# A hybrid attention layer on one core: the place of every instruction written down instead of found by priority

## The chip, the cores and the metric

The kernel runs on one core of a Trainium2 chip. The metric is the device time of one launch in microseconds (us), the median over several runs. The engines are TensorE (PE, matmuls and transposes; its weight loads are drawn apart as PEld), VectorE (DVE), ScalarE (ACT), GpSimd (POOL) and SyncE (SP), which only issues DMAs. Each engine has an instruction list of its own and takes it strictly in order; semaphores hold an instruction until what it needs is there.

## The reference

One layer on 1024 tokens of 1024 features. Cut to what is computed:

```python
h = rms_norm(x, norm_pre_g)
sb_q, sb_k, sb_v, sb_g, c_q, c_kv, k_rope, mla_g = split(h @ w_in)       # 1024 -> 2976
# group A, 8 heads of 64: stick-breaking attention, blocks of 128 queries, strictly causal
z = q_blk @ k.T * 64 ** -0.5
log_fail = where(past, log_sigmoid(-z), 0)
suffix = cumsum(log_fail, reverse=True) - log_fail
w = where(past, exp(log_sigmoid(z) + suffix), 0);  sb_o = w @ v
# group B, 8 heads: latent attention
q = rms_norm(c_q, q_norm_g) @ w_uq;  kv = rms_norm(c_kv, kv_norm_g) @ w_ukv
z = (q_nope @ k_nope.T + rope(q_rope) @ rope(k_rope).T) * 96 ** -0.5
mla_o = softmax(where(visible, z, -inf)) @ v
y = concat(head_rms_norm(sb_o) * silu(sb_g), head_rms_norm(mla_o) * silu(mla_g)) @ w_out
x = x + rms_norm(y, norm_post_g)
x = x + rms_norm(p @ w_ple, ple_norm_g) * sigmoid(x @ w_ple_gate + b_ple_gate)
```

Everything is float32.

## The kernel before

*Arithmetic and tiles.* A float32 product is made of three matmuls: each operand is split into a high part (a cast to the rounded type fp32r) and a low part (a subtraction), and high x high, high x low and low x high are added in one PSUM bank. So nearly every matrix that PE reads has first been cast (on ACT or DVE) and subtracted (on DVE or POOL). Matmuls are up to 512 columns wide; 128x128 transposes stand between them. q, k, v, the gates and other intermediate results go through DRAM scratch (`q_d`, `k_d`, `v_d`, `qr_d`, `gate_d`, `ple_d`), so a later stage reads by DMA what an earlier one stored.

*Stages.* The head (to about 20 us) loads x and the weights of v. Then come the projections by blocks of 128 tokens or 128 columns, woven with attention from about 65 us on. Attention is worked off in 16 rounds (`SEQ`: a head pair of one of the two groups, for one half), its matmuls woven with the remaining projections. From about 560 us on come the output projection, the second norm, and the last product with `w_ple_gate`, made by seven block products instead of eight; the tail is the last sum, sigmoid, product, addition and store of the output.

*What sets the order.* The kernel isn't written engine by engine. The calls of `block_kernel` go to a `Recorder`, which notes 6621 instructions with their dependences: PE 3905, SP 386 DMAs, the rest on DVE, ACT and POOL. `FLIP` is a list of numbers of such instructions that go to another engine than the text says (`other`): a `tensor_tensor` from DVE to POOL or back, a copy from ACT to DVE or back. `schedule` then plays the program through with estimated durations and gives each instruction a time; `issue` emits them in the order of those times, so that all of them have the same line in the profile (L754 before, L1069 after). The list that results is fixed when the kernel is built. Nothing is decided on the chip.

*Buffers.* Tiles come from pools that rotate: 28 places `u` and 10 places `f` of 4 KB per partition in SBUF, the four `h16`, and in PSUM 3 banks `a` (accumulators) and 5 banks `t` (transposes, scores). In the profile and in the rows below a tile is named by its place: `u_11` is the eleventh of `u`. A tile gets its place in `grant` in the order of the tiles' `turn`; a place is free when the last user of the earlier tile is done, a storing DMA included. So an instruction can wait for its inputs, for the engine that used its output's place before, or for the instructions ahead of it on its own engine.

*The priority before.* Of the instructions that are ready on an engine `schedule` takes the one with the lowest `prio`: its number in the program's text, plus a shift of its chunk (`SHIFT`, one pair of numbers for each piece of the program, the first for instructions and the second for tiles), plus `LOW` for the filling work, plus a bias.

Of the kernel before, what the change touches and what calls it, by code (L numbers as in the profile page):

```python
# [47 lines left out]
def f(ap):  # L48
# [4 lines left out]
LOW = 336  # L53
# [22 lines left out]
SHIFT = {  # L76
# [267 lines left out]
SETS = {AF.Sigmoid: "sig", AF.Exp: "exp", AF.Sin: "sin"}  # L344


class Recorder:
# [3 lines left out]
    def __init__(self, nc):  # L351
# [4 lines left out]
        self.low = False  # L356
        self.front = False
        self.bias = 0
        self.chunk = 0
        self.thread = ""  # L360
        self.threads = [""]

# [7 lines left out]
    def tile(self, pool, shape, dt, tag, slots, name, kind, part=None):  # L370
# [9 lines left out]
        key = t.tensor.name  # L380
# [19 lines left out]
    def turn(self, by=0):  # L400
        return len(self.ins) + SHIFT.get(self.chunk, (0, 0))[by]

# [1444 lines left out]
```

## Time and profile before

| | |
|---|---|
| time, median of 3 runs | 767.02 us (766.11 to 768.51) |
| the profiled execution | 765.48 us |
| its span in the trace | 763.7 us |
| PE busy | 751.0 us, 3905 matmuls and transposes |
| DVE, ACT, POOL busy | 630.6, 399.7, 321.7 us |
| DMA traffic | 148.71 MB, 195 GB/s over the span |
| granted clock of PE, mean | 0.999 |

The profiled execution lies 1.5 us below the median, and 1.8 us of it are outside the span that the trace shows. Busy times are sums of what each engine shows as running; a matmul is drawn from its start to a modelled end, so neighbours overlap and a short hold of PE inside a run doesn't appear as idle time. Idle time of an engine other than PE costs nothing by itself.

### The profile page before, as it was taken

How to read it: one execution, taken by the hardware profiler on the slowest of the kernel's cores; microseconds unless marked ns; L12 is line 12 of the kernel's file. 1: busy time of each engine (PE TensorE's matmuls, PEld its weight loads, DVE VectorE, ACT ScalarE, POOL GpSimd, SP SyncE). 2: the span in 40 equal slices, each digit the busy share in tenths (PEclk: the TensorE clock that was granted, in tenths of full speed). 3: DMA queues.
4: the chain of work that ended last, by engine and by line, in shares of the span. 5: the costliest groups of instructions: out<-in, count | busy, mean ns of one | idle time of the engine just before them, and what ended most of it. 6: DMA issues, size and time to landing. Idle time of an engine off the chain costs nothing.

```text
span 763.7 us, 11831 instructions
## 1 busy us (share of the span) xinstructions
PE 751.0 (98%) x3905; PEld 621.0 (81%) x3905; DVE 630.6 (83%) x1238; ACT 399.7 (52%) x962; POOL 321.7 (42%) x306
## 2 busy tenths in 40 slices
PE   7999999999999999999999999999999999999997
PEld 4888998878888878888887788888888888888876
DVE  6966355599958869888888999989899998789987
ACT  7633133244534785666657767767765541451221
POOL 2141113104411269869888521430363126464642
PEclk9999999999999999999999999999999999999999
DMA  9753103587998643656545884878436367272332
GB/s 324 247 168 129 74 33 120 190 313 279 341 355 272 214 132 137 198 189 209 175 138 162 270 298 145 286 267 286 144 116 212 125 248 244 87 276 83 110 111 83
DMA packets 101982, 148.71 MB, mean 195 GB/s; under 512 B 7448, under 2 KB 55072, under 8 KB 101920
## 3 DMA queue, kind: packets, MB, share of 16 engines
q1 hardware_dynamic: 101920, 147.95, 57.3%
q8 instruction: 31, 0.51, 0.3%
q14 instruction: 31, 0.25, 0.1%
HBM read 101.26 MB, written 46.66 MB: 194 GB/s over the span
## 4 chain that ended last, share of the span: by engine, by line
PE 88%; ACT 5%; DVE 3%; DMA 2%; issue 1%; POOL 0%; SPq 0%; ACTq 0%; DVEq 0%; POOLq 0%
PE a L754 62%; PE t L754 26%; ACT u L754 3%; DVE u L754 1%; DMA u<-k_d 1%; DMA v_d<-f 1%; ACT L754 1%; ACT h L754 1%; ACT f L754 1%; DVE nm L754 1%; DVE f L754 1%; DMA u<-v_d 0%; SPq L754 0%; DVE t L754 0%; DVE nms L754 0%
## 5 line engine op out<-in xcount | busy, mean ns | idle before, releaser
L754 POOL TENSOR_TENSOR u<-u,u 128x512 f32<-128x512 f32 (+14 forms) x134 | 190.5, 1436 | 140.1 <-ACT u L754 74.8
L754 PE MATMUL a<-h,f 128*128 128x512 f32 x864 | 240.7, 404 | 0.0
L754 PEld LDWEIGHTS a<-h,f 128*128 128x128 f32 x864 | 155.2, 189 | 26.4
L754 DVE TENSOR_TENSOR u<-t,u 128x512 fp32r<-128x512 f32 (+4 forms) x284 | 150.6, 555 | 22.2 <-ACT u L754 12.8
L754 PE MATMUL t<-u,u 128*128 128x512 f32 (+4 forms) x580 | 151.0, 367 | 1.0 <-DMA u<-k_d 0.5
L754 PE MATMUL a<-u,u 128*128 128x512 f32 (+2 forms) x522 | 133.4, 370 | 0.1
L754 PE MATMUL t<-ident,u 128*128 128x128 f32 (+1 forms) x793 | 126.4, 273 | 1.4 <-DVE nms L754 0.5
L754 ACT CAST u<-t 128x512 fp32r<-128x512 f32 (+3 forms) x192 | 87.4, 490 | 75.4 <-PE t L754 49.0
L754 PEld LDWEIGHTS t<-u,u 128*128 128x128 f32 x580 | 103.0, 189 | 20.2 <-ACT u L754 3.2
L754 PE MATMUL a<-h,u 128*128 128x512 f32 (+1 forms) x492 | 117.3, 391 | 0.1
L754 ACT ACTIVATE u<-t 128x512 f32<-128x512 f32 (+5 forms) x208 | 92.0, 515 | 47.2 <-PE t L754 38.6
L754 PEld LDWEIGHTS t<-ident,u 128*128 128x128 f32 (+1 forms) x793 | 97.1, 140 | 22.3 <-DVE u L754 2.9
L754 PEld LDWEIGHTS a<-h,u 128*128 128x128 f32 x492 | 89.6, 188 | 20.3 <-DVE u L754 0.5
L754 PEld LDWEIGHTS a<-u,u 128*128 128x128 f32 x522 | 91.7, 188 | 16.9 <-DVE u L754 2.0
L754 DVE TENSOR_TENSOR u<-u,u 128x512 fp32r<-128x512 f32 (+8 forms) x88 | 79.6, 917 | 5.3 <-ACT u L754 3.5
L754 ACT ACTIVATE u<-t,nms 128x384 f32<-128x384 f32 (+5 forms) x96 | 55.2, 581 | 39.7 <-DVE nms L754 39.4
L754 DVE TENSOR_TENSOR_SCAN u<-u 128x320 f32<-128x320 f32 (+4 forms) x64 | 64.6, 1011 | 13.6 <-ACT u L754 12.4
L754 ACT ACTIVATE f<-a 128x512 bf16<-128x512 f32 (+2 forms) x64 | 34.2, 539 | 51.5 <-PE a L754 48.4
L754 POOL MEMSET u<- 128x128 f32 x64 | 13.0, 216 | 102.1 <-PE a L754 56.4
L754 DVE TENSOR_TENSOR u<-a,u 64x512 f32<-64x512 f32 (+4 forms) x75 | 47.8, 647 | 8.2 <-ACT u L754 6.9
L754 DVE TENSOR_REDUCE nm<-t 128x1 f32<-128x384 f32 (+5 forms) x96 | 51.8, 547 | 1.9 <-PE t L754 1.2
L754 PE MATMUL a<-u,h 128*128 128x512 f32 x192 | 47.0, 399 | 1.5 <-ACT h L754 1.4
(111 smaller groups left out, 801.1 us busy)
## 6 DMA issues: line engine op xcount, KB each, us to landing
u<-q_d SPq DMA_DIRECT2D x64, 256.0 KB, 4.4
u<-k_d SPq DMA_DIRECT2D x16, 512.0 KB, 5.1
u<-v_d SPq DMA_DIRECT2D x16, 512.0 KB, 5.4
u<-in_w_ple_gate_dram SPq DMA_DIRECT2D x16, 512.0 KB, 6.7
f<-in_w_in_dram SPq DMA_DIRECT2D x14, 512.0 KB, 5.1
v_d<-u SPq DMA_DIRECT2D x12, 512.0 KB, 3.1
f<-in_x_dram SPq DMA_DIRECT2D x9, 512.0 KB, 4.4
q_d<-u SPq DMA_DIRECT2D x9, 512.0 KB, 4.4
```

The costliest lines, as they stand in the source:

```text
L754: x["fn"](*[place(a) for a in x["args"]], **{k: place(a) for k, a in x["kw"].items()})
```

## The change

`SHIFT` is empty. `FLIP` is a new list. `BASE` holds one number for each of the 6621 instructions, its place, and `TURNS` one for each tile of a rotating pool, its turn; both were found by a search that also played the program with transfers landing late. With `BASE` there, `schedule` no longer picks the lowest ready instruction: each engine's instructions are sorted by `BASE` and taken strictly in that order. No arithmetic, DMA or tile is added or removed.

```diff
-SHIFT = {
-    0: (1204, 1209), 1: (-381, -413), 2: (-586, -394), 3: (-857, -953), 4: (-1159, -1106), 5: (-11, -91),
...
+SHIFT = {}
 FLIP = (
...
+BASE = (
+    3, 5, 8, 4, 2, 6, 10, 7, 17, 18, 19, 21, 22, 24, 26, 28, 29, 33, 36, 38, 14, 15, 23, 57, 13, 16, 44, 87, 56, 60,
...
+TURNS = (
+    2, 18, 16, 17, 16, 81, 159, 162, 141, 189, 273, 274, 275, 161, 192, 182, 393, 378, 372, 142, 145, 71, 80, 80, 71,
...
-            self.tiles[key].update(turn=self.turn(1), turn0=len(self.ins), chunk=self.chunk)
+            self.tagged += 1
+            place = TURNS[self.tagged - 1] if TURNS else len(self.ins)
+            self.tiles[key].update(turn=place + SHIFT.get(self.chunk, (0, 0))[1], turn0=place, chunk=self.chunk)
...
-    def turn(self, by=0):
-        return len(self.ins) + SHIFT.get(self.chunk, (0, 0))[by]
+    def turn(self):
+        i = len(self.ins)
+        return (BASE[i] if BASE else i + (LOW if self.low else 0) + self.bias) + SHIFT.get(self.chunk, (0, 0))[0]
...
-                             chunk=self.chunk, prio=self.turn() + (LOW if self.low else 0) + self.bias, func=SETS.get(func) if op == "activation" else None))
+                             chunk=self.chunk, prio=self.turn(), func=SETS.get(func) if op == "activation" else None))
...
+        line = {e: sorted((i for i in range(n) if ins[i]["eng"] == e), key=lambda i: (-ins[i]["prio"], -i))
+                for e in engines}
         while done < n:
             best = None
             for e in engines:
-                if avail[e]:
+                if BASE:
+                    if not line[e] or need[line[e][-1]]:
+                        continue
+                    s = max(free[e], ready[line[e][-1]])
+                elif avail[e]:
...
-            while pend[e] and pend[e][0][0] <= s:
-                r, i = heapq.heappop(pend[e])
-                heapq.heappush(avail[e], (ins[i]["prio"], i))
-            _, i = heapq.heappop(avail[e])
+            if BASE:
+                i = line[e].pop()
+            else:
+                while pend[e] and pend[e][0][0] <= s:
+                    r, i = heapq.heappop(pend[e])
+                    heapq.heappush(avail[e], (ins[i]["prio"], i))
+                _, i = heapq.heappop(avail[e])
```

Between the two `FLIP` lists 253 instructions change engine: 76 from DVE to ACT, 62 from ACT to DVE, 62 from POOL to DVE, 53 from DVE to POOL. On PE the order moves only locally. Three places are spoken of below. A row gives the line, the operation, its output, its inputs and the output's shape.

*DVE at 65 to 82 us.* Here the weights of `c_load` (two 128-row blocks by 416 columns at a time, 832 columns in a row) are split; `128x832` with two inputs is the subtraction that makes a low part, and `128x4x64` are the casts and subtractions of `v_store`, whose result goes to `v_d`. Before:

```order
L754 SCALAR_TENSOR_TENSOR u_9_782<-u_9_782 128x256
L754 TENSOR_TENSOR u_22_792<-u_22_792 128x192
L754 SCALAR_TENSOR_TENSOR u_22_792<-u_22_792 128x192
L754 CAST f_7_815<-a_1_308 128x4x64
L754 TENSOR_TENSOR u_22_792<-u_22_792 128x382
L754 TENSOR_TENSOR f_7_815<-a_1_308,f_7_815 128x4x64
L754 CAST f_7_815<-a_1_308 128x4x64
L754 TENSOR_TENSOR f_0_826<-f_2_683,f_3_748 128x832
L754 TENSOR_TENSOR f_7_815<-a_1_308,f_7_815 128x4x64
L754 CAST f_8_840<-a_2_235 128x4x64
L754 TENSOR_TENSOR f_8_840<-a_2_235,f_8_840 128x4x64 x2
L754 CAST f_7_872<-f_2_834 128x832
```

The same place after:

```order
L1069 TENSOR_TENSOR f_1_752<-a_2_306,f_1_752 128x4x64 x2
L1069 TENSOR_TENSOR t_1_165<-t_1_165,mask_71 128x128
L1069 TENSOR_TENSOR t_2_173<-t_2_173,mask_71 128x128
L1069 TENSOR_TENSOR t_4_226<-t_4_226,mask_71 128x128
L1069 SCALAR_TENSOR_TENSOR u_14_764<-u_14_764 128x128
L1069 TENSOR_TENSOR f_1_800<-f_2_713,f_6_757 128x832
L1069 SCALAR_TENSOR_TENSOR u_18_783<-u_18_783 128x256
L1069 CAST f_7_813<-a_1_197 128x4x64
```

The subtraction (`f_0_826`, now `f_1_800`) has moved ahead of the scans of 256 and 192 columns (`SCALAR_TENSOR_TENSOR` in these rows) and of the casts of `v_store`, and the cast of the next block, `f_7_872` before, is no longer on DVE. The place `f_1` that it writes was the v tile `f_1_752`, which is being stored to `v_d`.

*PE at 434 to 439 us.* Transposes of softmax rows into `t` banks, and the wide matmuls of weights by values into an `a` bank. Before:

```order
L754 MATMUL t_2_224<-ident_66,u_21_4024 128x128
L754 MATMUL t_2_224<-ident_66,u_24_4101 128x128
L754 MATMUL t_2_224<-ident_66,u_26_4141 128x128
L754 MATMUL t_2_224<-ident_66,u_16_4185 128x128
L754 MATMUL t_1_216<-ident_66,u_24_4101 128x128
L754 MATMUL t_1_216<-ident_66,u_26_4141 128x128
L754 MATMUL t_1_216<-ident_66,u_16_4185 128x128
...
L754 MATMUL a_2_235<-u_27_4316,u_7_3965 128x512 x2
L754 MATMUL a_2_235<-u_20_4307,u_7_3965 128x512 x2
```

After:

```order
L1069 MATMUL a_0_128<-u_27_3815,u_26_4018 128x512
L1069 MATMUL t_2_173<-ident_66,u_4_4033 128x128
L1069 MATMUL t_2_173<-ident_66,u_14_4103 128x128
L1069 MATMUL a_0_128<-u_20_4227,u_26_4018 128x512
L1069 MATMUL t_2_173<-ident_66,u_13_4163 128x128
L1069 MATMUL t_2_173<-ident_66,u_18_4197 128x128
L1069 MATMUL t_0_180<-u_3_4236,u_8_2021 128x256
L1069 MATMUL t_0_180<-u_3_4236,u_20_4227 128x256
L1069 MATMUL t_0_180<-u_7_2023,u_0_4112 128x256
L1069 MATMUL a_0_128<-u_2_2036,u_26_4018 128x512
L1069 MATMUL t_1_165<-ident_66,u_14_4103 128x128
L1069 MATMUL t_1_165<-ident_66,u_13_4163 128x128
```

Value matmuls of the same accumulator, now in bank `a_0` instead of `a_2`, stand between the transposes of `t_2` and `t_1`; before they came after all of them.

*SP at 490 to 495 us.* Loads of a round of latent attention: parts of q (`q_d5`), of v (`v_d1`), of k (`k_d5`), the rotary part of q (`qr_d`), and other work's DMAs. Before:

```order
L754 DMA u_3_3224<-q_d5_91 128x512
L754 DMA u_4_4984<-v_d1_85 128x8x128
L754 DMA u_25_3756<-q_d5_91 128x1x512
L754 DMA u_11_4998<-k_d5_99 128x1024
L754 DMA u_13_4371<-qr_d_102 128x1x512
L754 DMA f_9_5016<-in_w_out_dram 128x2x512
L754 DMA gate_d5_109<-f_7_4538 128x512
```

After:

```order
L1069 DMA u_25_4969<-q_d5_91 128x1x512
L1069 DMA u_18_4976<-q_d5_91 128x512
L1069 DMA u_26_4994<-k_d5_99 128x1024
L1069 DMA u_25_4969<-qr_d_102 128x1x512
L1069 DMA f_9_5006<-in_w_out_dram 128x2x512
L1069 DMA gate_d5_109<-f_0_4658 128x512
L1069 DMA u_0_5036<-v_d1_85 128x8x128
```

The load of v has gone from second place to the last of the seven, and k is third.

More of the change, by code (lines that the diff above doesn't have):

```diff
@@ L74 @@
 AHEAD = 52
-SHIFT = {
[160 rows of a table removed]
-}
-FLIP = (
[11 rows of a table removed]
+SHIFT = {}
+FLIP = (
[13 rows of a table added]
+)
+BASE = (
[341 rows of a table added]
+)
+TURNS = (
[114 rows of a table added]
 )
@@ L359, in __init__ @@
         self.chunk = 0
+        self.tagged = 0
         self.thread = ""
```

636 rows, old and new, of tables (BASE, FLIP, SHIFT, TURNS) are left out of this document.

## The prediction

> **What bounds the kernel now.** I read the head of the page first: the span, the busy engines, the clock and the chain that ended last.
>
> ```profile
> span 763.7 us, 11831 instructions
> PE 751.0 (98%) x3905; PEld 621.0 (81%) x3905; DVE 630.6 (83%) x1238; ACT 399.7 (52%) x962; POOL 321.7 (42%) x306
> PE 88%; ACT 5%; DVE 3%; DMA 2%; issue 1%; POOL 0%; SPq 0%; ACTq 0%; DVEq 0%; POOLq 0%
> ```
>
> TensorE (PE) is busy for 98% of the span and carries 88% of the chain, so a new order can only gain what PE spends standing. How much is that? The windows say where it is plain to see.
>
> ```profile
> 0.00:100.00 100.00, 95.32 (x455) 77.70 (x456) 60.98 (x163) 45.04 (x135) 20.69 (x33) 1.00 0.53 180
> 400.00:500.00 100.00, 97.52 (x544) 80.83 (x543) 93.18 (x220) 70.35 (x181) 44.15 (x41) 1.00 0.71 237
> 700.00:764.00 64.00, 58.54 (x276) 47.73 (x274) 54.48 (x79) 15.15 (x26) 30.72 (x22) 0.98 0.28 100
> ```
>
> After the name and length of a window stand PE, PEld, DVE, ACT and POOL, then the granted clock, 1.00 here. PE idles 763.7 - 751.0 = 12.7 us: 4.7 in the first hundred, 2.5 between 400 and 500, 5.2 in the last window up to the end of the span, and 0.3 in all the rest. That is a lower bound, since a matmul held up for a tenth of a microsecond is still drawn as busy. The upper bound is a count at the unstalled pace, which the chain gives in one long row.
>
> ```profile
> 660.07 23.18 PE a L754 x100
> 683.25 0.55 PE t L754 x5
> ```
>
> The hundred are 512 columns wide: 0.232 us each; a transpose takes 0.11. All forms of matmul, first and last of the 26 rows of that view:
>
> ```profile
> L754 PE MATMUL a<-h,f 128*128 128x512 f32 x864 | 240.7, 404 | 0.0
> ...
> L754 PE MATMUL t<-ident,u 8*128 8x8 f32 x1 | 0.2, 223 | 0.0
> ```
>
> Added up over the 26 rows, 2196 matmuls are 512 wide (509 us), 768 are 256 to 448 wide (123 us in proportion to width), 929 are 128-wide transposes, mask additions and one small one (101 us), and 12 in the head are slow (5.24 us, below): about 738 us, an estimate. The next rows show that the first matmul starts at 2.21 and the last ends at 757.74 + 0.86 = 758.60.
>
> ```profile
> 2.21 5.24 PE a L754 x12
> ```
> ```profile
> 757.74 0.86 PE L754 MATMUL a<-h,u 128*128 128x256 f32 x6
> 758.21 0.93 POOL L754 TENSOR_TENSOR u<-u,u 128x256 f32<-128x256 f32 x1 [0.87 <-ACT u L754]
> 758.64 0.42 DVE L754 TENSOR_TENSOR u<-a,u 128x256 f32<-128x256 f32 x1
> ```
>
> 758.6 - 2.2 - 738 leaves 18 us of standing between first and last matmul, plus 5.1 us of tail. Three or four of the 18 are the head, where weights and x have yet to arrive. So 12 to 14 us is all that any order can take from the middle, most of it in pieces of 0.1 to 0.5 us. Hence I look for the few places with a stall of about one microsecond and ask whether the new order cures them, and what it exposes instead.
>
> **The change, part by part.** Nothing is computed that was not computed before; PE runs the same 3905 matmuls. Every engine executes its list in order, before and after, so what changes is who stands behind whom.
>
> *1. The c_q/c_kv weight at 65 to 82 us (removed: 1.0 us).*
>
> ```profile
> 73.35 1.01 DVE L754 TENSOR_TENSOR f<-f,f 128x832 fp32r<-128x832 f32 x1
> ```
> ```profile
> 74.43 0.38 SPq L754
> ...
> 74.91 6.39 DMA v_d<-f
> ...
> 81.40 0.60 DVE f L754
> ```
> ```profile
> DVE f L754 <- DMA v_d<-f: 5.2, 2, 4.6
> PEld a L754 <- DVE f L754: 1.0, 1, 1.0
> ```
>
> The low part of the first weight block is taken late on DVE (73.35 to 74.36). Only then is its raw buffer free, so the next block's load goes out at 74.43 and the store of v behind it at 74.91. The store lands at 81.30, DVE splits the next block at 81.40, and PE loses 1.0 us. The new order has that subtraction 11 places earlier on DVE, right behind a scan, and gives the next block's cast to ACT. What then holds the subtraction is the landing of an earlier store of v, whose buffer it takes. That store went alone:
>
> ```profile
> GB/s 412 437 409 384 313 209 45 30 0 0 0 0 0 0 0 89 387 447 432 417 134 0 0 0 0 0 0 0 0 0 0 0 0 0 0 0 0 0 0 0
> ```
>
> This is the traffic from 62 to 73 us in 40 slices: the store's packets fill slices 16 to 21, from 66.1 to 67.8. Its four pieces are made later in the new order, by about 1.9 us when I lay the durations of before along the new DVE and ACT rows, so it lands near 69.7. The load then goes out near 71 instead of 74.4 and the second store near 74, which gives 3 us against a stall of 1.0. Between bounds: 0 if the earlier store lands late, -1.0 if not. I take -1.0.
>
> *2. The attention stage at 434 to 438.6 us (removed: 1.4 us).*
>
> ```profile
> 435.47 0.66 PE L754 MATMUL t<-ident,u 128*128 128x128 f32 x4 [0.22 <-DVE u L754]
> 436.67 0.55 PE L754 MATMUL t<-ident,u 128*128 128x128 f32 x3 [0.54 <-DVE nms L754]
> 437.54 0.39 PE L754 MATMUL t<-u,u 128*128 128x256 f32 x1 [0.32 <-ACT u L754]
> ...
> 438.59 2.58 PE L754 MATMUL a<-u,u 128*128 128x512 f32 x10
> ```
> ```profile
> 436.59 0.68 DVE L754 TENSOR_TENSOR f<-a,f 128x512 f32<-128x512 f32 x1
> ...
> 437.85 0.68 DVE L754 TENSOR_TENSOR f<-a,f 128x512 f32<-128x512 f32 x1
> ```
>
> Seven transposes of two softmax rows follow each other at the pace at which DVE and ACT make the rows: 0.22 + 0.54 + 0.32 = 1.08 us idle in the drawing, 1.6 us if the starts are laid against the pace of 0.11 per transpose. Eight wide value matmuls then stand ready but behind, because their accumulator's bank is freed only by the DVE addition at 437.85. In the new order the accumulator has another bank, freed by the addition that was at 436.59, which now stands earlier on DVE, and six of the eight stand between these transposes: 6 x 0.232 = 1.39 us of work over a wait of 1.6. I take -1.4. The other bound is +0.5: if that addition is still late, the first wide matmul waits and with it all transposes behind it.
>
> *3. The load of k at 491 to 499.5 us (removed: 0.8 us).*
>
> ```profile
> 491.11 0.55 SPq L754 DMA_DIRECT2D u<-v_d  x1
> ...
> 492.47 0.53 SPq L754 DMA_DIRECT2D u<-k_d  x1
> ```
> ```profile
> 492.47 6.85 DMA u<-k_d
> ...
> 499.46 1.55 PE t L754 x10
> ```
> ```profile
> PEld t L754 <- issue: 0.8, 1, 0.8
> ```
>
> The load of v (512 KB) stands before k in the queue though v is used well after k. The new order puts v behind k, the rotary queries, a weight of w_out and a gate store. k then goes out near 491.2, 1.3 us earlier, with 512 KB less ahead of it; either alone covers the stall of 0.8. v becomes late instead: issued near 494 and needed after 510, it has 16 us for a transfer that took k 6.85. I take -0.8; bounds 0 and -0.8.
>
> *4. Swaps of engine.* 76 casts go from DVE to ACT and 62 back, 62 products and subtractions from POOL to DVE and 53 back. DVE's count stays nearly the same, but the mix moves with the stage. Prices of the products between 280 and 400 us:
>
> ```profile
> L754 DVE TENSOR_TENSOR u<-t,u 128x512 fp32r<-128x512 f32 x23 | 14.7, 680 | 1.9 <-ACT u L754 1.9
> L754 DVE TENSOR_TENSOR u<-u,u 128x512 fp32r<-128x512 f32 x6 | 8.6, 1429 | 1.3 <-ACT u L754 1.3
> ```
> ```profile
> L754 POOL TENSOR_TENSOR u<-u,u 128x512 f32<-128x512 f32 x10 | 17.8, 1788 | 0.6 <-DMA u<-gate_d 0.5
> ```
>
> With one input in PSUM the operation takes 0.68 us on DVE, with both in SBUF beside a busy POOL 1.43. A product moved from POOL to DVE costs DVE 0.68 to 1.43 us, frees POOL of 1.79 and shortens what DVE runs beside it. Between 280 and 400 this adds about 9 us to DVE by count; DVE has idle time there, and from 560 on, where it is fuller, the swaps take 6 to 7 us off it per hundred. I count the swaps as -1.0 us on the small stalls, between -5 (a third of the 14 us) and +3 (nine products moved to DVE from 685 us on, each late by a third of a microsecond).
>
> The Trainium skill ("SBUF — State Buffer", Who interferes with whom) states that a DVE operation with two SBUF inputs and a GpSimd operation that reads SBUF exclude each other for the whole instruction. The pair 680 and 1429 agrees: 0.75 us is what one such meeting costs here. The rule speaks against the moves to POOL late in the kernel; that case is rival d.
>
> *5. Head and tail (added: 0.5 us).* In the head the casts of the first v weights swap ACT and DVE and x's first block is loaded second rather than fourth. The first weight's low part comes about 1 us later and PE has caught up by 20 us: 0, within 0.6 either way. In the tail the last 256-wide product goes from DVE to POOL. POOL took 0.93 for such a one in the row at 758.21, and DVE 0.42 for an operation as wide at 758.64: +0.5, on the path, since the sum and the store of the output stand behind it.
>
> *Sum.* -1.0 - 1.4 - 0.8 - 1.0 + 0.5 = -3.7 us on a profiled execution of 765.5 us, of which the span is 763.7 and 1.8 lies around it. The median of the runs shown is 767.0, 1.5 us above; I count from the median: 763.3, rounded to 763.
>
> **The rivals.** *a. The stalls move (same).* DVE is the second engine throughout: 93.18 us busy between 400 and 500, with PE behind it all the time. An order fixed in advance may cure three places and open three others of the same size. One I can name: at 688 us.
>
> ```profile
> 687.10 1.21 DVE L754 TENSOR_TENSOR h<-u,h 128x1024 fp32r<-128x1024 f32 x1
> ```
> ```profile
> 688.47 1.55 PE a L754 x6
> ```
>
> That split ends at 688.31 and PE needs it 0.16 us later; one product of 0.68 moved from POOL ahead of it is a new stall of 0.5. With part 1 still stalled (1.0), half of part 2 lost (0.7) and this, 3.7 shrinks to 1.5: 765.5.
>
> *b. The small stalls go too (faster by more).* If DVE's relief takes 6 of the 12 to 14 us in the middle, the time is 767 - 2.7 - 6 = 758. [...]
>
> *c. DVE stands behind a late store (slower).* The subtraction of part 1 is now early on DVE, and waits for the store of v. The two later stores to the same place took longer than the lone one:
>
> ```profile
> v_d<-f SPq DMA_DIRECT2D x2, 512.0 KB, 6.0
> ```
>
> Issued at 67.4, a store of 6.0 lands at 73.4, and DVE, otherwise there at about 70, stands for 3 us with scans, mask additions and the v casts of PE's next projection behind it. This decides from a landing after 71, where DVE's own lateness begins to reach PE. Part 1 then turns from -1.0 to +2 or +3, the block behind is later by as much again, and with parts 2 and 3 only half as good the time is 767 + 5 - 1.1 = 771. Against it: no other transfer is in flight at 67, as the traffic row shows.
>
> *d. POOL's products hold DVE up at the end (same).* From 685 us on, by count of the two orders, 14 products go from DVE to POOL and 9 the other way, 5 more for POOL. If each of the 14 meets a DVE operation on two SBUF tiles, DVE loses 14 x 0.75 = 10.5 us there, and the 9 moved the other way give back 6.8. The 3.7 us that remain come on PE only if DVE is what PE waits for after 685; the last window, with DVE at 54.48 of 64, has little room. All of it on PE gives 763.3 + 3.7 = 767. Against it: each product that leaves also takes its own 0.68 us off DVE, 3.4 us net. By the Trainium skill ("SBUF — State Buffer", Who interferes with whom) each such meeting is one in which one side stands still.
>
> **How the numbers follow.** A comparison of this kernel tells 0.3%, 2.3 us, from no change: faster is below 764.7, slower above 769.3. My forecast, 761 to 764.7 with 763.0 in its middle: 0.42. Rival b, 757 to 761: 0.18. Rival a, 764.7 to 769.3: 0.19; rival d, in the same bracket: 0.07. Rival c, above that: 0.14. So faster 0.60, same 0.26, slower 0.14. The range 757 to 769 holds the forecast, a, b and d and leaves out c and the end of b beyond 757; the likeliest case's own range is 761 to 764.7.
>
> **What would show it.** Right: no wait of DVE for a store of v near 80 us and no stall of PE there; wide matmuls between the transposes near 433 us with no idle time of half a microsecond; k landing before PE asks for it near 497; PE's busy time down by 1 to 2 us and its idle time between 400 and 500 near 1.0 instead of 2.5. Wrong: a wait of DVE for a store near 70 us longer than 1 us (c), or new PE waits for DVE of 0.5 us or more between 560 and 760 (a). The tail after the last matmul should be 5.5 us instead of 5.1; if it is not, part 5 is mispriced.

## The result, and the profile after

The kernel after the change takes 775.49 us (median of 4 runs, 773.68 to 775.96) against 766.76 for the kernel before on the same chip. The ratio is 1.0107, with 1.0093 to 1.0121 as its 95% interval: slower by 8.7 us, where I forecast 763 and gave slower a chance of 0.14. The profiled execution, the fastest of the four, took 773.68 us. The head of its page:

```profile
span 771.9 us, 11765 instructions
PE 749.8 (97%) x3905; PEld 620.1 (80%) x3905; DVE 612.2 (79%) x1233; ACT 409.0 (53%) x974; POOL 306.2 (40%) x297
```

The work is the same and even looks lighter: DVE is busy 18.4 us less than before, POOL 15.5 less. PE idles 771.9 - 749.8 = 22.1 us in the drawing instead of 12.7. The windows (PE, PEld, DVE, ACT, POOL, then the granted clock) say where:

```profile
0.00:100.00 100.00, 95.84 (x469) 79.34 (x470) 57.22 (x167) 46.90 (x143) 27.47 (x38) 1.00 0.52 180
300.00:400.00 100.00, 98.02 (x540) 79.84 (x539) 81.98 (x127) 61.25 (x129) 66.39 (x55) 1.00 0.52 171
400.00:500.00 100.00, 95.31 (x531) 78.50 (x529) 95.39 (x213) 71.82 (x183) 40.94 (x42) 1.00 0.72 235
500.00:600.00 100.00, 98.65 (x556) 83.31 (x555) 89.26 (x182) 68.59 (x161) 34.18 (x35) 1.00 0.58 194
600.00:700.00 100.00, 96.36 (x474) 79.28 (x473) 82.63 (x132) 39.09 (x82) 42.36 (x31) 0.98 0.54 184
700.00:772.00 72.00, 66.00 (x312) 53.80 (x310) 54.22 (x76) 21.34 (x38) 38.70 (x28) 0.98 0.28 99
```

The first hundred is 0.5 us better than before. From 300 on it is worse: 2.0 us idle between 300 and 400, 4.7 between 400 and 500 (2.5 before), 1.4 and 3.6 in the next two, where before there was 0.3 in all. Against the prediction's estimate of 738 us for all matmuls at the unstalled pace, PE stands 25.8 us between the start of its first and the end of its last matmul (2.25 and 766.00); counted in the same way the kernel before stands 18.4. Whom it waits for stands in the view of PE's waits, the first three rows of after, then the same kinds of wait in the kernel before (us in total, times, longest):

```profile
PE a L1069 <- DVE u L1069: 3.9, 4, 2.0
PE t L1069 <- DVE u L1069: 3.1, 6, 0.8
PE a L1069 <- DVE f L1069: 2.8, 3, 1.2
```
```profile
PE a L754 <- DVE f L754: 1.0, 2, 0.7
...
PE t L754 <- DVE u L754: 0.4, 2, 0.2
```

So a DVE that has less to do makes PE wait 9.8 us for its `u` and `f` tiles instead of 1.4. The reason can be read where the loss is densest, 420 to 440 us. First PE's largest stalls there, then DVE's list, then POOL's, all of after:

```profile
423.64 0.73 PE L1069 MATMUL a<-f,f 128*128 128x512 f32 x2 [1.23 <-DVE f L1069]
...
430.67 0.51 PE L1069 MATMUL a<-f,f 128*128 128x512 f32 x1 [0.96 <-DVE f L1069]
...
439.08 0.50 PE L1069 MATMUL a<-u,u 128*128 128x512 f32 x1 [0.57 <-DVE f L1069]
```
```profile
421.56 1.69 DVE L1069 TENSOR_TENSOR hsm<-hss 128x1 f32<-128x1 f32 x1
...
428.17 1.85 DVE L1069 TENSOR_TENSOR hsm<-hss 128x1 f32<-128x1 f32 x1
429.94 0.68 DVE L1069 TENSOR_TENSOR f<-a,f 128x512 f32<-128x512 f32 x1
...
437.14 1.23 DVE L1069 TENSOR_TENSOR hsm<-hss 128x1 f32<-128x1 f32 x1
...
438.35 0.67 DVE L1069 TENSOR_TENSOR f<-a,f 128x512 f32<-128x512 f32 x1
```
```profile
421.46 1.77 POOL L1069 TENSOR_TENSOR u<-u,u 128x894 f32<-128x894 f32 x1 [1.09 <-DVE u L1069]
...
428.00 2.00 POOL L1069 TENSOR_TENSOR u<-u,u 128x1022 f32<-128x1022 f32 x1 [0.68 <-issue]
...
437.07 1.29 POOL L1069 TENSOR_TENSOR u<-u,u 128x512 fp32r<-128x512 f32 x1 [5.03 <-ACT u L1069]
```

The three DVE operations with one column each (`hsm`, a sum of two numbers per partition for the norm of `p @ w_ple`) take 1.69, 1.85 and 1.23 us. Each starts 0.07 to 0.17 us after a POOL product that reads two SBUF tiles, and each ends with it: 423.25 and 423.23, 430.02 and 430.00, 438.37 and 438.36. The kernel before has the same sum beside the same product (DVE, then POOL):

```profile
420.93 0.15 DVE L754 TENSOR_TENSOR hsm<-hss 128x1 f32<-128x1 f32 x1
```
```profile
421.02 1.77 POOL L754 TENSOR_TENSOR u<-u,u 128x894 f32<-128x894 f32 x1
```

There the sum starts 0.09 us ahead and takes 0.15. Who starts first by a tenth of a microsecond decides over 1.5 us of DVE, and DVE takes its list in order: behind the held sums stand the additions `f<-a,f` that free PE's accumulators. The kernel before has held sums too, 2 of 16 (after: 4 of 16); its next one, beside another product of POOL, is one of them:

```profile
424.40 1.18 DVE L754 TENSOR_TENSOR hsm<-hss 128x1 f32<-128x1 f32 x1
```

It ends with that product (425.58 and 425.57), and PE is busy all the time from 424.40 to 435, so a hold costs only where PE waits for DVE next. The Trainium skill ("SBUF — State Buffer", Who interferes with whom) says that whoever issues first has the shared pair of ports for the whole instruction and that issue order, not the shape, decides who blocks; the three rows of after agree, with ends equal within 0.02 us.

The same thing at 684 us, first DVE, then POOL, then PE:

```profile
684.59 3.42 DVE L1069 SCALAR_TENSOR_TENSOR f<-f,hsr,f 128x1024 f32<-128x1024 f32 x1
```
```profile
684.44 2.49 POOL L1069 TENSOR_TENSOR h<-u,h 128x1024 fp32r<-128x1024 f32 x1 [1.04 <-ACT h L1069]
```
```profile
689.99 0.73 PE L1069 MATMUL a<-u,u 128*128 128x512 f32 x2 [2.02 <-DVE u L1069]
...
691.36 3.56 PE L1069 MATMUL a<-u,u 128*128 128x512 f32 x8
```

DVE is held for 2.3 us (POOL ends at 686.93), PE stands 2.0, and eight matmuls behind it take 3.56 us, where the same eight take 2.09 in e4 below: the granted clock has dropped, to half for 3.41 us (the last section has its rows).

### The profile page after: what moved, and what is told of

The parts are those of the page before. It is cut to its first block, busy times and chain, and to the rows that moved or that the text cites. A ratio compares the mean times of both kernels' runs of the same rounds, so it can differ in the third digit from the quotient of the medians.

```text
span 771.9 us, 11765 instructions
## 1 busy us (share of the span) xinstructions
PE 749.8 (97%) x3905; PEld 620.1 (80%) x3905; DVE 612.2 (79%) x1233; ACT 409.0 (53%) x974; POOL 306.2 (40%) x297
## 5 line engine op out<-in xcount | busy, mean ns | idle before, releaser
L1069 PE MATMUL a<-h,f 128*128 128x512 f32 x864 | 260.0, 409 | 0.0
L1069 POOL TENSOR_TENSOR u<-u,u 128x512 fp32r<-128x512 f32 (+14 forms) x137 | 187.4, 1379 | 173.6 <-ACT u L1069 88.8
L1069 PE MATMUL t<-u,u 128*128 128x512 f32 (+4 forms) x572 | 165.8, 369 | 1.3 <-DVE u L1069 0.9
L1069 PE MATMUL a<-u,u 128*128 128x512 f32 (+2 forms) x521 | 148.6, 379 | 5.0 <-DVE u L1069 3.2
L1069 PE MATMUL t<-ident,u 128*128 128x128 f32 (+1 forms) x793 | 146.2, 273 | 3.6 <-DVE u L1069 2.1
L1069 PE MATMUL a<-h,u 128*128 128x512 f32 (+1 forms) x492 | 127.7, 396 | 0.0
L1069 DVE TENSOR_TENSOR u<-u,u 128x512 f32<-128x512 f32 (+14 forms) x94 | 82.0, 881 | 10.0 <-POOL u L1069 4.7
L1069 DVE TENSOR_TENSOR_SCAN u<-u 128x320 f32<-128x320 f32 (+5 forms) x64 | 55.9, 878 | 13.7 <-ACT u L1069 12.8
L1069 ACT ACTIVATE f<-a 128x512 bf16<-128x512 f32 (+3 forms) x64 | 34.2, 538 | 52.1 <-PE a L1069 49.7
L1069 DVE TENSOR_TENSOR f<-a,f 128x512 f32<-128x512 f32 (+2 forms) x54 | 34.4, 644 | 18.0 <-ACT f L1069 14.7
```

Source lines behind the costliest of these rows:

```text
L1069: x["fn"](*[place(a) for a in x["args"]], **{k: place(a) for k, a in x["kw"].items()})
```

## The experiments

My theory: the new list lets POOL's products hold DVE at places where PE needs DVE next ("meetings"). The rivals: the order itself puts something needed behind something late, whatever POOL does; or curing one place moves everything behind it, so that new stalls open far away; or the swaps of engine load DVE too much (its busy time speaks against that already). All medians in one table; "standing" is the time in the profiled run from the start of PE's first to the end of its last matmul, less the 738 us, so an estimate.

| kernel | us | before, beside it | ratio (95%) | standing |
|---|---|---|---|---|
| before | 766.76 | | | 18.4 |
| after | 775.49 | 766.76 | 1.0107 (1.0093 to 1.0121) | 25.8 |
| e1 old, new order at the three places | 768.88 | 767.52 | 1.0027 (1.0014 to 1.0040) | 21.4 |
| e2 old, new order at 400 to 450 us | 778.43 | 767.52 | 1.0148 (1.0132 to 1.0164) | 30.6 |
| e3 old, new order from 620 us | 773.29 | 767.52 | 1.0077 (1.0063 to 1.0091) | 24.0 |
| e4 new, three sums on POOL | 768.70 | 767.52 | 1.0027 (1.0014 to 1.0039) | 20.4 |
| e5 e4 and two moves | 769.12 | 767.08 | 1.0026 (1.0015 to 1.0037) | 21.0 |
| e6 e5 and seven more | 767.97 | 767.08 | 1.0005 (0.9995 to 1.0015) | 20.7 |
| e7 new, POOL's products short | 764.98 | 767.08 | 0.9967 (0.9955 to 0.9978) | 18.4 |
| e8 old, POOL's products short | 765.74 | 767.08 | 0.9984 (0.9975 to 0.9993) | 19.7 |
| e9 old, two cures by hand | 766.19 | 766.58 | 0.9992 (0.9981 to 1.0002) | 19.1 |
| e10 old order, new swaps | 790.58 | 766.58 | 1.0326 (1.0309 to 1.0342) | 42.2 |
| e11 new order, old swaps | 791.49 | 766.58 | 1.0327 (1.0306 to 1.0349) | 45.8 |
| e12 e9 and two more moves | 765.38 | 766.60 | 0.9984 (0.9973 to 0.9994) | 19.3 |

The numbers of instructions in the diffs are those of the program's text.

### e1: the three places of the prediction alone

```diff
-BASE, TURNS, FLIP: the old order throughout
+new order and swaps for what stands at 62-102, 430-441 and 480-505 us, the old order elsewhere
```

> The old order with three stretches of the new one, cut out and set in: 62 to 102 us (the c_q/c_kv weights), 430 to 441 us (value matmuls between the transposes) and 480 to 505 us (k ahead of v). The places, swaps of engine and tile turns inside the stretches are those of the new order; the rest is the old one. By the steps of the prediction: -1.0, -1.4 and -0.8 against the old kernel, about 763.6 us, and no stall of PE of over 0.3 us near 81, 436 and 499 us. Rival (the stalls only belong to how late each engine is when it comes there, so a cure of one order does not carry over): no change within 0.7 us, 766 to 767.5.

Measured: slower by 0.27%, where the prediction's parts 1 to 3 would have made it faster by 3 us. The windows, first of e1, then of the kernel before for the third row:

```profile
60.00:100.00 40.00, 40.00 (x206) 36.80 (x205) 13.90 (x43) 11.64 (x44) 7.04 (x9) 1.00 0.23 84
420.00:440.00 20.00, 18.53 (x103) 15.03 (x104) 18.39 (x50) 14.38 (x40) 11.70 (x13) 1.00 0.71 231
600.00:640.00 40.00, 37.40 (x200) 30.56 (x199) 35.33 (x66) 17.67 (x42) 10.32 (x7) 1.00 0.47 164
```
```profile
420.00:440.00 20.00, 18.69 (x101) 14.41 (x101) 18.15 (x47) 15.22 (x41) 10.62 (x12) 1.00 0.80 267
```

The place at 65 to 82 us is cured, and so is the one at 491 (PE busy 19.90 of the 20 us from 480 on); the one at 434 is not. And 2.6 us are lost between 600 and 640, where the list is the old one. There DVE waits 2.00 us for PE to give up the buffer place that it is to write, and PE then 1.29 us for what stands behind it on DVE:

```profile
613.51 0.43 DVE L977 COPY u<-rs 128x512 f32<-128x512 f32 x1 [2.00 <-PE t L977]
```

The other 1.1 us of the third row stand at 629, where PE waits behind a cast for the first load of `w_ple_gate`; e9 below has the same place. The tiles behind a splice take other places in the rotation, so a wait for a place can open where nothing was changed, here 108 us behind the last splice. That is the mechanism of the prediction's rival a.

### e2 and e3: one stretch of the new order at a time

```diff
-BASE, TURNS, FLIP: the old order throughout
+e2: new order and swaps for what stands at 400-450 us, the old order elsewhere
+e3: new order and swaps for what stands from 620 us on, the old order ahead of it
```

> The old order with the new one only between 400 and 450 us. Theory of the meetings: the new order lets a product on GpSimd start just ahead of DVE operations on two SBUF tiles here (at 416, 419, 421, 426, 428 and 437 us), DVE stands until the product ends, and PE waits behind it. That belongs to this stretch: PE loses 2 to 3.5 us more than in the old order, 769 to 770.5 us, and additions of one column take over 1 us on DVE again. Rival (the stretch is only the victim of lateness built up before 400 us): within 0.7 us of the old kernel.

> The old order until 620 us and the new one from there to the end. If the late stalls of the new order are made by its own late part: +1.5 at about 630, +2.2 at about 682, and +1.6 of matmuls at 0.427 us instead of 0.232 behind the second, so about 772 us, with a granted clock near 0.91 in the 20 us around the second. If they are handed down from earlier stretches: 766 to 768 us and no dip of the clock.

Inside its stretch e2 shows the six stalls of after, and PE is idle 2.4 us more there than in the kernel before. That part came as expected, but the total missed the expectation by some 8 us, since the list behind the stretch no longer fits: PE is idle for 2.51 us at 462, 1.09 at 473 and 1.24 at 508, where neither parent has an idle time of that size. In e2, with a drop of the clock (the kernel before has 29.92 of 30 us busy here):

```profile
450.00:480.00 30.00, 26.26 (x135) 21.25 (x134) 23.22 (x61) 16.37 (x48) 5.98 (x7) 0.94 0.51 173
```

So e2 can't say what 400 to 450 costs in the whole, only that its stalls are its own. e3 has the later of after's two late stalls (2.09 us at 688), without the drop of the clock, so the late part makes it itself. The other (1.30 at 635 in after) isn't there; instead PE stands 1.28 at 614, ahead of the splice, and 1.02 at 625. Splicing is a poor knife for a list of this kind: both halves change.

### e4: the three sums taken out of the way

```diff
 FLIP = (
+    3543, 3623, 3703: the three one-column sums of 421 to 438 us, on POOL instead of DVE
 BASE
+    3703 right behind 3790
```

> The new order with three additions of one column (the sums of squares of the embedding branch, which took 1.69, 1.85 and 1.23 us on DVE at 421.6, 428.2 and 437.1 us) moved from DVE to GpSimd. Their work is 0.14 us each. Theory of the meetings: DVE no longer stands behind three products, the stalls of 1.4 us at 422, 1.1 and 0.5 at 430 and 0.7 at 438 shrink by half or more, 772 to 773.5 us against 775.5. Rival (DVE is simply full there and what stands ahead of PE's work does not matter): 0.3 to 0.5 us, 775.

POOL takes its own list in order, so a sum on POOL can't meet a product on POOL. Three instructions out of 6621, of 0.14 us each, give back 6.8 us by the medians and 6.1 by the ratios, of 8.7 and 8.2: more than expected. Every engine's list is otherwise that of after; 237 of the 2184 rotating tiles get another place, since places were not held here. Windows of after and of e4:

```profile
420.00:440.00 20.00, 16.42 (x87) 12.31 (x86) 19.62 (x37) 12.14 (x32) 8.92 (x9) 1.00 0.62 196
```
```profile
420.00:440.00 20.00, 19.39 (x111) 16.06 (x112) 18.47 (x46) 15.32 (x40) 12.17 (x20) 1.00 0.79 255
```

PE does 111 matmuls instead of 87 in these 20 us. The addition that after runs at 429.94 now stands here:

```profile
426.01 0.67 DVE L978 TENSOR_TENSOR f<-a,f 128x512 f32<-128x512 f32 x1
```

3.9 us earlier. Two of the three sums stood ahead of it, and by the starts behind them they took 1.61 and 1.77 us of DVE's list; a 512-wide subtraction `u<-u,u` at 425.05 also takes 0.66 us where it took 1.71 beside POOL at 426.16, another meeting gone; against that e4 comes into the stretch 0.5 us later. The stall near 686 is still there (2.06 us), but without the drop of the clock, which is a part of the gain: the eight matmuls behind it take 2.09 us.

```profile
687.38 2.09 PE L978 MATMUL a<-u,u 128*128 128x512 f32 x8
```

### e5 and e6: more stalls cured one by one

```diff
 e5, on e4:
+BASE: 5671 just ahead of 5728 (the stall at 634 us); 6040 just behind 6056 (the one at 688)
 e6, on e5:
+FLIP: 3501 and 4023 on POOL
+BASE: 3181 behind 3170, 4400 and 4401 behind 4670, 2796 ahead of 2828, 3501 behind 3684
 both: every tile keeps the buffer place that it had in the new order
```

> The kernel with the three additions on GpSimd (768.7 us), its buffer places held at those of the new kernel, and two operations moved on DVE: at 634 us the addition that reads the output projection's bank goes ahead of a subtraction that waits for a cast of ACT (DVE stands idle there with the addition ready behind), and at 688 us the 1024-wide residual operation that took 3.42 us beside a product on GpSimd goes behind the sums that PE waits for. Theory of the meetings and of work ready behind a waiting head: -1.4 and -2.2, about 765 us. Rival (these stalls come from how full DVE is): the same stall comes back at the next operation, 767.5 to 769.

> As the one with two more moves, and five more of the same kind: a fourth one-column addition (462 us) on GpSimd; the subtraction that was held 1.1 us at 416 us on GpSimd; at 319 us a cast that PE waits for ahead of a scan that a product holds; at 360 us a scan behind the addition that PE waits for; at 515 us a 1024-wide cast that was held 2.2 us (with the subtraction that follows it on GpSimd) behind what PE waits for. By the theory each gives its stall of 0.5 to 1.4 us, 5 us in all: 760 us, or 762.5 if half of them open others; below the old kernel in either case. Rival: no better than 765.

Both missed, and came out about where their rivals stood. In e5 the stall at 634 is gone and the one at 686 falls from 2.06 us to 0.88 and 0.46, but 0.73 opens at 526 and 0.92 at 640: nothing is gained in all. e5 differs from e4 by more than its two moves: it takes the 237 tiles back to their places in the new order, and two of the sums have other ranks in POOL's list. In e6 every stall that I aimed at is smaller or gone (1.18 falls to 0.60 at 516), 0.89 is left at 685, and 0.71 and 0.64 open at 222 and 428. Between e5 and e6 the places are the same, so it isn't they that move the stalls there; I didn't find out which meetings or transfers take over in each case.

### e7 and e8: the suspected cause made small everywhere

```diff
+    if x["eng"] == "POOL" and x["op"] == "tensor_tensor" and len(args[0].shape) == 2 and args[0].shape[-1] >= 256:
+        self.POOL.eng.memset(args[0].bitcast(F32), 0.5)
+        args = [a[:, 0:64] if isinstance(a, bass.AP) else a for a in args]
```

> The new kernel in which each GpSimd product of 256 columns or more is cut to its first 64 columns, after a memset that fills the whole tile (so work is left out and the values are others): GpSimd then reads two SBUF tiles for some 0.2 us instead of 1.3 to 2.5. Order and places as in the new kernel. Theory of the meetings: DVE's holds vanish, and with them some 10 us or more of PE's stalls: 762 to 766 us, within 2 us of the old kernel so cut. Rival (the new order leaves DVE too little room, whatever GpSimd does): 772 us or more, and 6 us or more above the old kernel so cut.

> The old kernel with the same cut of GpSimd's products (work left out, values others). Theory of the meetings: the old order has as many meetings but few of them ahead of what PE waits for, so it gains little, 2 to 4 us: 763 to 765. Rival (both orders lose alike by meetings): it gains as much as the new one, 756 to 758.

The list and every wait stay as they were; POOL's products of the plain two-dimensional form are shortened, those of other forms not (the 1022-column product and the 512-column one at 437 us among them). The new order gains 10.5 us, the old one 1.3; the 8.7 us between the two become -0.8. The busy engines, e7 and then e8:

```profile
PE 748.3 (98%) x3905; PEld 618.8 (81%) x3905; DVE 593.5 (78%) x1233; ACT 408.5 (54%) x974; POOL 255.4 (33%) x385
```
```profile
PE 751.5 (98%) x3905; PEld 621.2 (81%) x3905; DVE 599.5 (78%) x1238; ACT 399.8 (52%) x962; POOL 265.4 (35%) x395
```

Nothing was taken off DVE, and yet its busy time falls by 18.7 and 31.1 us: that is time in which POOL had held it. The old order was held for longer and lost 1.3 us by it, less than the 2 to 4 expected; the new one was held for less and lost more than the 8.7 us between the two. What e7 can't separate is that short products are also ready sooner; e4, in which no product got shorter, can. Two of the three sums are still held in e7 (1.84 and 1.23 us, by the products that were not cut), and PE nonetheless works 18.73 of the 20 us there: DVE comes to them 4 us earlier, since the operations ahead of them are no longer held.

### e9 and e12: the cures of parts 1 and 3 in the old order

```diff
 e9, old order, buffer places held:
+DVE: 633, the subtraction of part 1, right behind the scan at 67.6 us
+SP: 4512, the load of v, behind the loads of k and the rotary queries (4516)
 e12, on e9:
+ACT: 5706, a cast, behind 5626;  DVE: 5707, its subtraction, behind 5706
```

> The old order with two operations moved and nothing else, the buffer places held word for word at the old ones: on DVE the subtraction of the first c_q/c_kv weight goes right behind a scan at 67.6 us (11 places earlier), on SP the load of v goes behind k and the rotary queries at 491 us. These are parts 1 and 3 of the prediction alone. By its steps -1.0 and -0.8: 765.2 us against the old kernel's 767. The three-places kernel cured both and lost 2.7 us at 613 and 629 us, where its order is the old one; there DVE waited for a buffer place that another tile had held in the old kernel. If that is the cause, with the places held these two stalls do not appear, 765 to 765.8. Rival (any shift of DVE and GpSimd against each other throws the later meetings anew, places or not): stalls of 1 us or more turn up behind, 766.5 to 769.

> The old order with the two cures (subtraction of the first c_q/c_kv weight earlier on DVE, v behind k on SP) and two more moves, places held: the cast and the subtraction of the first w_ple_gate block, which ACT and DVE took at 622.7 and 623.8 us in the two-cures kernel, go behind the copy and the product that the output projection waits for. Their matmuls come only at 674 us. In the two-cures kernel the load of that block landed 8.5 us after its issue instead of 6.7; ACT waited 2.7 us for it with everything behind, and PE stood 1.8 us at 626. If a head of the line that waits for a transfer is what ate the two cures, PE no longer stands there: 764.3 to 765.3 us, faster than the old kernel by 0.2 to 0.3%. Rival (the meetings behind are thrown anew and take it back): 766 or more, with stalls of 1 us at other places behind 626 us.

Windows of the kernel before, then of e9:

```profile
60.00:100.00 40.00, 39.32 (x199) 35.85 (x198) 16.28 (x45) 10.11 (x38) 5.59 (x8) 1.00 0.23 80
...
560.00:640.00 80.00, 79.79 (x434) 67.10 (x433) 75.10 (x150) 39.92 (x95) 25.34 (x26) 1.00 0.51 170
```
```profile
60.00:100.00 40.00, 40.00 (x204) 36.81 (x203) 16.89 (x47) 10.88 (x44) 6.27 (x8) 1.00 0.21 80
...
560.00:640.00 80.00, 78.13 (x425) 65.68 (x424) 73.66 (x147) 39.90 (x94) 25.14 (x24) 1.00 0.51 166
```

Both places are cured, worth 0.7 us in the first row and 0.3 between 480 and 510 (29.48 busy before, 29.80 now), and the median moves by 0.4, which its interval doesn't tell from nothing: 1.7 us are lost at 628. With the places held e1's wait at 613 is gone; this one is not. Here PE waits behind a cast for the first load of `w_ple_gate`. Everything has come about 1.1 us ahead, the load too, which goes out at 614.18 instead of 615.32; but its cast starts at 622.72 instead of 622.06. First the kernel before, then e9: the load's issue and the cast.

```profile
615.32 7.87 SPq L754 DMA_DIRECT2D u<-in_w_ple_gate_dram  x8
```
```profile
622.06 1.05 ACT L754 CAST u<-u 128x1024 fp32r<-128x1024 f32 x1 [0.90 <-DMA u<-in_w_ple_gate_dram]
```
```profile
614.18 7.85 SPq L3164 DMA_DIRECT2D u<-in_w_ple_gate_dram  x8
```
```profile
622.72 1.05 ACT L3164 CAST u<-u 128x1024 fp32r<-128x1024 f32 x1 [2.70 <-DMA u<-in_w_ple_gate_dram]
```

8.5 us from issue to use instead of 6.7, with the same eight loads issued in a row. That the load is slower for being earlier isn't shown: in e8, where SP's and ACT's lists are the old ones, it goes out at 615.92 and is used at 624.42, 8.5 us too (PE loses 0.65 there). Its time spreads from one kernel to another, and why stays open. e12 takes the operations that depend on that cast out of PE's way, and is the fastest version of the real computation: 765.38 against 766.60 for the kernel before beside it (0.9984, 0.9973 to 0.9994), just above what I expected. In its profiled run, its slowest, a stall of 1.0 us is left at 629. What a cure is worth is set by what is late next.

### e10 and e11: order and swaps crossed

```diff
 e10: BASE and buffer places of the old order
-    FLIP: the old list
+    FLIP: the new list
 e11: BASE and buffer places of the new order
-    FLIP: the new list
+    FLIP: the old list
```

> The old order and the old buffer places, but with the new list of swaps between engines (253 instructions run on the other engine, at their old rank). If the swaps bring the meetings (62 products and subtractions more on DVE among them), this is 772 us or more and its DVE holds lie ahead of PE's work at 415 to 440 us as in the new kernel. If order and swaps were fitted to each other, both crossings are slower than either fitted kernel, 776 to 785. If the order alone is the cause, 765 to 768.

> The new order and the new buffer places, with the old list of swaps. If the swaps bring the meetings: 765 to 769 us. If order and swaps were fitted to each other: 778 to 785, above the new kernel. If the order alone is the cause: 774 to 777 as the new kernel.

The crossings are 24 and 25 us slower than the kernel before, more than expected. PE's longest kind of wait, e10 and then e11:

```profile
PE t L3165 <- DVE u L3165: 5.2, 11, 1.2
```
```profile
PE a L3164 <- DVE u L3164: 7.3, 12, 2.6
```

So neither table does with the other's partner, which speaks for their having been fitted to each other. "The swaps" have no price of their own: the new list costs 8.7 us with its own order and 24 with the other one.

## Why the prediction was wrong

*Part 4 is the step that failed.* I took the swaps as -1.0 us, between -5 and +3, by what they add to DVE and take off it. On DVE's load I was half right: from 560 to 700 it fell by 9.1 us, the 6 to 7 per hundred that I had counted, but between 280 and 400, where I had counted 9 us more, it fell by 2.6. And the price isn't in the sum of meetings; it is in where they fall. With parts 1 and 3 by the idle time of PE that went (-0.7, -0.5) and part 5 as it measured (+0.8), the rest of the change, parts 2 and 4, costs 8.7 + 0.7 + 0.5 - 0.8 = 9.1 us, against upper bounds of 0.5 and 3. I had the mechanism and its price, 0.75 us a meeting, and used it in rival d for the stretch from 685 us on, with a chance of 0.07. There it came (3.42 us for an operation, 2.0 us of PE's idle time); but the largest loss was at 416 to 438, where I counted no meeting, and the operations held were one-column sums that I had costed at nothing since they take 0.15 us. A held operation costs what is left of the product that holds it, up to 1.7 us for the sums, not its own length. e4 and, with the limit named there, e7 and e8 show it.

*Part 2 failed, by the same cause.* The six wide matmuls do stand between the transposes now, but the addition that frees their bank ran at 438.35, behind a held sum, and by then DVE was late (at the addition of 429.94 by the 3.9 us of e4). My upper bound, "if that addition is still late, the first wide matmul waits", is what happened (439.08, 0.57 us). In e1, where DVE isn't late from before, the same piece still gains nothing (18.53 against 18.69 us): there a transpose waits for DVE and another for a load. So the -1.4 was wrong even without the meetings.

*Parts 1 and 3 were right at their places, and priced too high.* I took 1.0 and 0.8 from the waits of PE's weight loads (PEld); PE's own idle time in these windows of 20 us was 0.68 and 0.52 before. Windows of after:

```profile
80.00:100.00 20.00, 20.00 (x113) 19.57 (x112) 6.60 (x28) 5.93 (x34) 4.26 (x6) 1.00 0.01 1
...
480.00:500.00 20.00, 20.00 (x116) 17.39 (x114) 19.28 (x48) 15.45 (x34) 7.04 (x7) 1.00 0.93 316
```

No idle time of PE in either. DVE does wait for the stores of v as rival c had it (`DVE f <- DMA v_d<-f`, 3.8 us between 60 and 100), but PE shows nothing of it. k went out at 494.14 instead of near 491.2, since PE is 4.5 us behind by 480 (11.2 us idle by then, 6.8 before); v no longer goes ahead of it, and that was enough. What failed is that a cured stall was counted in full to the end. e1 and e9 show it worth less or nothing in the total: 1.0 us cured by e9 is a median 0.4 lower, with 1.7 us of new stall at 628.

*Part 5 was close.* The tail is 5.9 us instead of 5.1 (+0.8, forecast +0.5). The last sum on DVE starts at 768.72, 0.62 us after DVE was free, since it waits for a 256-column operation on POOL of 0.83 us.

*The rivals.* Rival a had new stalls where old ones go, which came, and half a microsecond as the size of one; they measured 0.5 to 2.0, and the end was outside its bracket. The result lies above 769.3, in the bracket of rival c, but that is luck: c's sign came, waits of 1.09 and 2.67 us for the store at 68.87 and 78.90, and PE shows no idle time behind them. For the cause that decided I had no chance above 769.3. PE's busy time fell by 1.2 us as I said it would; that says nothing of the span, since PE's idle time grew by 9.4.

*What is open.* Why the cures in e5 and e6 don't add up, place by place. How much of the 8.7 us, and of the 6.8 that e4 gives back, the drop of the clock carries: it stands in the one profile that I have of after, where it takes about 1.5 us, and not in that of e4. How much the other places of e4's tiles do. And the stalls between 300 and 400 us, and two for ACT (1.22 at 518, 1.30 at 635), which no experiment addressed by itself.

## What to carry to other kernels

Where a long operation of one engine holds operations of another, look for short operations that start just behind a long one of the other engine, on the engine that the bound engine waits for next; the total of such meetings says little, and a held one-column sum can take as long as the wide product that holds it. In a list fixed in advance a cured stall is worth what is late next, so its full size is the bound and not the forecast, and an order, its engine assignment and its buffer places are to be tried together. When an operation is written into such a list, put it on the engine whose own list keeps it apart from the long one.

## What the hardware showed that I had not expected

- A DVE sum of 128x1 took 1.85 us instead of 0.14, and with 0.09 us of lead the same sum took 0.15. A scan of 448 columns and a three-input operation of 1024 columns were held in the same way (2.07 instead of 1.08 us, and 3.42).
- The clock dropped to half after a stall of PE of 2.02 us in after, but not after stalls of 2.09 and 2.06 us in e3 and e4. What tells them apart is where the stall lies against a fixed grid of 3.41 us. The stretches at half clock last 3.41 us or twice that inside the kernels, and they begin whole multiples of it apart (in after at 691.15 and, in the tail, 769.65: 23 x 3.413). Laid back from there, the windows of after, then the one of e3 that holds most of its stall and the one behind it:

```profile
687.74:691.15 3.41, 1.39 (x9) 0.95 (x8) 3.38 (x7) 2.18 (x2) 0.00 (x0) 1.00 0.72 292
691.15:694.56 3.41, 3.41 (x12) 2.74 (x11) 3.37 (x4) 1.71 (x3) 1.61 (x1) 0.50 0.00 0
```
```profile
685.97:689.38 3.41, 1.72 (x10) 1.10 (x8) 3.38 (x4) 0.95 (x1) 0.74 (x1) 1.00 0.96 357
689.38:692.79 3.41, 3.01 (x16) 2.49 (x17) 3.37 (x6) 2.95 (x4) 0.06 (x1) 1.00 0.33 132
```

  The whole stall of after lies in one window (2.02 us idle of 3.41); that of e3 is cut into 1.69 and 0.40, that of e4 into 0.80 and 1.26. In all 14 traces every window with 1.86 us or more of idle time is followed by one at half clock (2.51 in e2, 1.95 in e11), and of the windows at full clock none with 1.75 or less is (1.75 in e10, 1.68 in e9). So the idle time in one window decides here, and whether a stall of 2 us falls into one is a matter of where it lies.

  The Trainium skill ("TensorE: Matmul & The Clock Gate", What's actually happening) has the clock halved after at least one idle window of about 3.4 us and calls the window free-running. The traces agree on the length and on the fixed grid; they differ on the idle time, of which about 1.9 us in the window was enough here, and the measurement decides.
- One and the same load, issued with the same seven others behind it, was used 6.7 us after its issue in the kernel before and 8.5 us after it in e8 and e9.
